# Spreading the per-block preparation of an S5 scan mixer over other pairs of groups

## Chip, cores and metric

The kernel runs on one core of a Trainium2 chip. The metric is the time of one execution in device microseconds (us). Shown is the median of three runs of the kernel before, and beside it one profiled execution with its own time and trace.

## The reference, cut to what matters

One inference step of a two-layer backbone runs over 1024 sample tokens and 128 prompt tokens with 1024 channels. Layer 0 mixes the tokens with a state-space scan (S5): the 1024 channels are 64 groups of 16, each with 64 complex states and two directions.

```
lam = lax.complex(lam_re, lam_im); dt = exp(log_dt)[:, None]
abar = exp(lam * dt)
bbar = ((abar - 1.0) / lam)[..., None] * bmat
bu = einsum('blgc,gpc->blgp', u, bbar)        # plus abar*h0 at the edge
h = associative_scan(h[t] = abar * h[t-1] + bu[t])     # per direction
y_d = real(einsum('gcp,blgp->blgc', cmat, h))
out = gated(gelu(y_0 + y_1 + ssm_d * u))
```

Behind it come a ConvFFN, a Fourier mixer (layer 1) and another ConvFFN. The change touches the S5 mixer alone, which is the first 305 us of some 2409.

## The kernel before

**Tiling.** `Ssm.run` works on 8 blocks `b` of 128 channels (8 groups each). A block has 4 pairs `pr` of two groups, so there are 32 steps, `i = 4*b + pr`. Time is cut into frames of 8 tokens: within a frame the recurrence is unrolled into matrices, and only the frame states are scanned. For each block the kernel needs

- `u` (`make_u`, `load_u`): the normed input of the block. TensorE transposes and scales token tiles of `xb` in three parts (L1487): part 0 is the prompt tile with one matmul, parts 1 and 2 are four sample tiles each. ScalarE writes them into one buffer `hb` (L1491, and L1495 and L1496 for two edge columns in part 0). Eight DMAs on the SP queue then read all of `hb` into `u` (L1502). There is only one `hb` and only one `xb`; `load_x` fills `xb` by DMA (L1341).
- `PT` (`make_p`): input matrices. Small factor products (L1418, L1423) and sums (L1429) are made on GpSimd, in block 1 on VectorE; TensorE transposes them, two transposes per half (L1437), and ScalarE copies them out (L1440). A half of `PT` serves two pairs.
- `CA` and `Bb` (`make_ca`): output matrices on GpSimd (L1359 to L1373), factors of the input on GpSimd (`bb[0]`) and VectorE (`bb[1]`, L1386 to L1396), edge copies on ScalarE (`ends`, L1377 to L1400).
- `T` (`make_t`): the kernel matrix inside a frame. TensorE makes it with 32 small matmuls (L1459, 64 rows by 32 columns, 128 wide; each shows as two instructions) into two banks, ScalarE copies it out (L1469 to L1471), GpSimd adds a diagonal (L1472, L1473), one DMA stores it to DRAM (L1475), and eight DMAs load it back skewed (L1478). These nine are on the SP queue too.
- `sn` and `cs` (`tables`): phases on VectorE (L1307, L1308, L983, L984), absolute value, sine and cosine on ScalarE (L1313, L1321).
- In block 0 alone, the powers and phases of all later blocks (`powers(rest, [second])`, shown under L951, with copies into `Q` and `G` on ScalarE, L1169 to L1173).

**Order.** The order on every engine is written out by hand: each engine and the SP queue take their instructions in program order, with waits that follow from the data and the buffers. Step `i` issues

1. `vmm(i+1)`: 16 matmul instructions of the next pair into one of two `V` buffers (L1515); it can start once step `i-1` has read that buffer (L1568);
2. a part of `make_u`, and in pair 0 `load_x`;
3. `scan(i)` on VectorE (L1556), `vin(i+1)` (L1537 to L1539 on VectorE, then four small ScalarE writes, L1541 to L1546, without which the next scan can't start), `vout(i)` (L1567, L1568), `decay(i+2)` on ScalarE (L1551);
4. `wmm(i-1)`: output matmuls with `T` (L1578) and `CA` (L1584), copied out by ScalarE (L1590);
5. the lists `fill` and `late`, in which the preparation of the next blocks is spread over the pairs.

In blocks 0 and 1 `vmm` also carries a slice of the adaLN projection (`ada_mm`, L1252, 32 instructions that walk over four column groups); its ScalarE copy `m_ada` (L1257) is one that L1537 of the same pair waits for.

The SP queue keeps eight DMA semaphores in turn, so a DMA is issued only when the one eight before it has landed. Before the change, block `b` does this:

```
pr 0: make_u(b+1) part 2, load_x(b+2), load_u(b+1), products half 0, tables s0, ends
pr 1: products half 1, transposes of half 0, wrap, abs, sine
pr 2: make_u(b+2) part 0, bb[0], CA 0..2, make_t(b+1) whole with its store and loads, cosine
pr 3: make_u(b+2) part 1, bb[1], CA 3..4, transposes of half 1
```

Of the kernel before, what the change touches and what calls it, by code (L numbers as in the profile page):

```python
# [12 lines left out]
AF = mybir.ActivationFunctionType  # L13
# [951 lines left out]
class Ssm:  # L965
# [478 lines left out]
    def make_t(self, b):  # L1444

        nc, sp, E = self.nc, self.sp, self.nc.gpsimd
        CA, Bb = self.CA[b], self.Bb[b]
        T = sp.tile([128, 8, 128], F32, tag="T", bufs=2, name="T")
        kc = self.sg.tile([128, 2, 240], F32, tag="kc", bufs=1, name="kc")
        k0 = self.sg.tile([128, 2, 16], F32, tag="k0", bufs=1, name="k0")  # L1450
        self.T[b] = T

        p = [self.bank("misc", 2) for _ in range(2)]
        for j in range(4):
            for a in range(2):
                rows = slice(64 * a, 64 * a + 64)
                for dr in range(2):
                    for ri in range(2):
                        nc.tensor.matmul(p[a][32 * j:32 * j + 32, dr * 128:dr * 128 + 128],  # L1459
                                         lhsT=Bb[rows, ri, 2 * j + dr].rearrange("p a b -> p (a b)"),  # L1460
                                         rhs=CA[rows, ri, 2 * j + dr, 2 * dr:2 * dr + 8].rearrange("p a b -> p (a b)"),
                                         start=ri == 0, stop=ri == 1)
        return lambda: self.store_t(b, p, T, kc, k0)

    def store_t(self, b, p, T, kc, k0):
        nc, sp, E = self.nc, self.sp, self.nc.gpsimd
        A = nc.scalar.activation
        for a in range(2):
            A(kc[:, a, 0:128], p[a][:, 128:256], AF.Copy)  # L1469
            A(k0[:, a], p[a][:, 0:16], AF.Copy)  # L1470
            A(kc[:, a, 128:240], p[a][:, 16:128], AF.Copy)  # L1471
        E.tensor_tensor(k0, k0, self.DD[:, b], OP.add)  # L1472
        E.tensor_tensor(kc[:, :, 112:128], kc[:, :, 112:128], k0, OP.add)  # L1473
        o = self.kd.offset + b * 2 * 128 * 240
        nc.sync.dma_start(bass.AP(tensor=self.kd.tensor, offset=o, ap=[[240, 128], [128 * 240, 2], [1, 240]]), kc)  # L1475
        for t in range(8):
            src = bass.AP(tensor=self.kd.tensor, offset=o + (7 - t) * 16, ap=[[240, 16], [32 * 240, 8], [1, 128]])
            nc.sync.dma_start(T[16 * t:16 * t + 16], src)  # L1478
# [125 lines left out]
    def run(self):  # L1604
# [3 lines left out]
        call = lambda fs: [f() for f in fs]  # L1608
        rest = slice(16, NG)
# [38 lines left out]
        ca1, ends1, bb = self.make_ca(1)  # L1648
        call(bb)
        self.diagonal()  # L1650
        self.make_t(0)()
        self.loads(2)
        n = 32
        for i in range(n + 1):
# [4 lines left out]
            if pr == 0 and n1 and b:  # L1659
                self.make_u(b + 1, parts=(2,))  # L1660
                if n2:
                    self.load_x(b + 2)
            elif pr > 1 and n2:
                self.make_u(b + 2, parts=(pr - 2,))
            if i < n:
                self.scan(i)
            if i + 1 < n:
# [14 lines left out]
                self.made.__exit__(None, None, None)  # L1682
            fill, late = [], []
            if pr == 0:
                if n1 and b:
                    self.load_u(b + 1)
                if b:
                    self.store_y(b - 1)
                if n1:
                    pp, tr = self.make_p(b + 1)  # L1690
                    fill = list(pp[0])
                    if b:
                        tb = self.tables(b + 1)
                        fill += tb[:1]
                if n1 and b:
                    late = [ends]
                if not b:
                    self.make_u(1)
                    self.load_u(1)
                    self.load_x(2)  # L1700
                    tb = self.tables(1)
                    fill += tb[:2] + ca1
                    second = Later(self.nc.vector)
                    self.phases(second, rest)
                    self.phases16(second, rest)
                    late = tr[0] + tb[2:3] + [lambda: self.powers(rest, [second]), ends1]
            if pr == 1:
                if n1:
                    fill = list(pp[1])
                    late = tr[0] + tb[1:3] if b else tb[3:]  # L1710
                if n2:
                    if b + 3 < 8:
                        self.loads(b + 3)
            if pr == 2:
                if n1:
                    late = [lambda: self.make_t(b + 1)()]
                    if b:
                        late += tb[3:]
                if n2:
                    ca, ends, bb = self.make_ca(b + 2)  # L1720
                    bb[0](self.nc.gpsimd if b else self.nc.vector)
                    fill = ca[:3]
            if i == 7:
                late = [self.last_frame]
            if pr == 3 and n1:
                late += tr[1]
                if n2:
                    bb[1]()
                    fill = ca[3:]
            if i >= 27:  # L1730
                late.append(lambda: self.n.early(i - 27))
            call(fill)
# [157 lines left out]
```

## Time and profile before

| | us |
|---|---|
| median of three runs (2411.02 to 2411.6) | 2411.51 |
| the profiled execution's own time | 2410.76 |
| its span, first to last instruction | 2408.9 |
| TensorE busy over the span | 2284.9 (95%) |
| VectorE busy over the span | 1469.9 (61%) |
| mixer loop, scan of step 0 to the last output matmul | 45.8 to 305 |

The profiled execution is 0.75 us below the median; 1.9 us of its time lie outside the span. Busy shares over the whole span belong mostly to the FFN stages; what a change in the mixer is worth has to be read from the mixer's own stretch. Rows of a timeline give start, duration, engine, line, operation, output and inputs, count, and in brackets the idle time just before and what ended it. PEclk is the granted TensorE clock as a share of 2.4 GHz.

### The profile page before, as it was taken

Reading aid. Unit: us, or ns where it says so; the run is one execution under the profiler, and the core shown is the slowest. Engines: PE = TensorE matmul, PEld = TensorE weight load, DVE = VectorE, ACT = ScalarE, POOL = GpSimd, SP = SyncE. Lnnn points to the kernel's source line nnn. Section 1 sums busy time; section 2 is a strip of 40 time slices with the busy share of each in tenths; the row PEclk is TensorE's granted clock in tenths of the full one; section 3 lists DMA queues with packets and bytes.
Section 4 is the critical chain, followed back from the end, with each engine's and each line's share of the span. In section 5 each row is a group of like instructions: output and inputs, shape, how many; then the busy total and the mean of one; then the engine's idle time right before and its main releaser. Section 6 shows DMA issues by size and latency. Waiting matters only on the chain.

```text
span 2408.9 us, 35526 instructions
## 1 busy us (share of the span) xinstructions
PE 2284.9 (95%) x14658; PEld 2207.7 (92%) x14658; DVE 1469.9 (61%) x2327; ACT 879.4 (37%) x1352; POOL 726.9 (30%) x486
## 2 busy tenths in 40 slices
PE   4788899999999999999999999999999999999996
PEld 4677797879999999999999999999999999999996
DVE  8888868895654556445553664764456455554556
ACT  5566653235232223322232354542223322232234
POOL 6588412363221122211221254521112211221124
PEclk9899999999999999999999999999999999999998
DMA  6443496661111111111110131121011101111112
GB/s 221 121 95 91 114 322 225 216 217 32 49 53 36 36 35 53 45 36 35 44 53 27 53 108 36 48 68 36 27 44 53 44 27 44 44 53 36 36 36 79
DMA packets 94520, 182.31 MB, mean 76 GB/s; under 512 B 16948, under 2 KB 57204, under 8 KB 93336
## 3 DMA queue, kind: packets, MB, share of 16 engines
q1 hardware_dynamic: 90824, 170.67, 22.9%
q0 software_dynamic: 2096, 6.62, 0.8%
q8 instruction: 116, 1.90, 0.3%
q10 hardware_dynamic: 1440, 2.75, 0.3%
q14 instruction: 44, 0.36, 0.0%
HBM read 163.70 MB, written 11.53 MB: 73 GB/s over the span
## 4 chain that ended last, share of the span: by engine, by line
PE 73%; DVE 17%; issue 4%; DMA 3%; ACT 2%; POOL 1%; SPq 1%; DVEq 0%; ACTq 0%; POOLq 0%
PE acc L199 64%; DVE c L308 3%; PE f L199 3%; PE f L839 2%; DVE dh L602 2%; DVE dl L602 2%; DMA w_ada<-w_ada 1%; PE misc L1459 1%; PE f L749 1%; DVE X L363 1%; DMA X<-xT 1%; PE y L1584 1%; DVE V L1538 1%; DVE X L364 1%; DVE V L1539 1%
## 5 line engine op out<-in xcount | busy, mean ns | idle before, releaser
L199 PE MATMUL acc<-h,uh 128*128 128x384 f32 (+1 forms) x4992 | 1014.0, 338 | 0.5 <-ACT ysb L1590 0.5
L199 PEld LDWEIGHTS acc<-h,uh 128*128 128x128 f32 x4992 | 884.2, 188 | 14.2 <-issue 10.9
L183 POOL TENSOR_TENSOR ul<-raw,uh 128x1024 fp32r<-128x1024 f32 x104 | 279.5, 2688 | 1232.1 <-ACT uh L182 1232.1
L199 PE MATMUL acc<-h,ul 128*128 128x384 f32 (+1 forms) x2496 | 571.3, 337 | 0.0
L308 DVE SCALAR_TENSOR_TENSOR c<-t,cw,c 128x896 f32<-128x896 f32 x704 | 347.2, 562 | 202.4 <-ACT c L305 202.4
L199 PEld LDWEIGHTS acc<-h,ul 128*128 128x128 f32 x2496 | 448.3, 189 | 0.0
L182 ACT ACTIVATE uh<-raw 128x1024 fp32r<-128x1024 f32 x108 | 113.7, 1053 | 549.6 <-PE acc L199 495.8
L300 DVE COPY wb<-acc 128x2 f32<-128x2 f32 x88 | 13.9, 158 | 405.8 <-PE acc L199 405.8
L363 DVE SCALAR_TENSOR_TENSOR X<-acc,MOD,X 128x768 f32<-128x768 f32 x168 | 169.8, 1010 | 118.3 <-PE acc L199 118.3
L199 PE MATMUL acc<-gh,dh 128*128 128x384 f32 x960 | 220.8, 337 | 18.4 <-DVE X L365 18.4
L199 PE MATMUL acc<-gl,dh 128*128 128x384 f32 x960 | 218.6, 335 | 0.0
L199 PE MATMUL acc<-gh,dl 128*128 128x384 f32 x960 | 218.3, 335 | 0.0
L199 PEld LDWEIGHTS acc<-gh,dh 128*128 128x128 f32 x960 | 168.8, 188 | 26.9 <-PE acc L199 23.6
L336 ACT ACTIVATE gh<-c 128x1152 fp32r<-128x1152 f32 x44 | 51.4, 1169 | 329.2 <-DVE c L331 290.9
L199 PEld LDWEIGHTS acc<-gh,dl 128*128 128x128 f32 x960 | 171.4, 188 | 0.0
L199 PEld LDWEIGHTS acc<-gl,dh 128*128 128x128 f32 x960 | 171.2, 188 | 0.0
L303 ACT ACTIVATE t<-t,wb 128x1024 f32<-128x1024 f32 x88 | 101.4, 1153 | 152.5 <-DVE t L301 152.5
L183 POOL TENSOR_TENSOR dl<-raw,dh 128x1024 fp32r<-128x1024 f32 x40 | 99.8, 2515 | 165.0 <-ACT dh L182 165.0
L305 ACT ACTIVATE c<-t,cb,cw 128x1152 f32<-128x1152 f32 x88 | 118.9, 1351 | 2.9
L301 DVE TENSOR_TENSOR t<-acc,R 128x1152 f32<-128x1152 f32 x88 | 118.6, 1348 | 0.0
L326 ACT ACTIVATE c<-c 128x1152 f32<-128x1152 f32 x44 | 51.4, 1167 | 152.3 <-DVE c L308 152.3
L602 DVE SCALAR_TENSOR_TENSOR dl<-w_ada,SC,dl 128x1024 f32<-128x1024 f32 x50 | 88.9, 1816 | 0.0
(316 smaller groups left out, 2601.6 us busy)
## 6 DMA issues: line engine op xcount, KB each, us to landing
raw<-w_up SPq DMA_DIRECT2D x88, 512.0 KB, 3.6
w_ada<-w_ada SPq DMA_DIRECT2D x80, 512.0 KB, 4.9
raw<-w_down SPq DMA_DIRECT2D x44, 512.0 KB, 3.6
w_ada<-w_ada SPq DMA_DIRECT2D x8, 1024.0 KB, 5.9
raw<-w_glu SPq DMA_DIRECT2D x16, 512.0 KB, 4.6
u<-hb SPq DMA_DIRECT2D x64, 73.0 KB, 3.7
y_scratch<-ysb SPq DMA_DIRECT2D x8, 584.0 KB, 3.7
xt<-x SPq DMA_DIRECT2D x9, 512.0 KB, 8.1
```

What stands on the lines that cost most here:

```text
L182: nc.scalar.activation(hi, raw, AF.Copy)
L183: (E or nc.gpsimd).tensor_tensor(lo, raw, hi.bitcast(F32), OP.subtract)
L199: mm(outs[j], lhsT=w, rhs=r[j], start=first and i == 0, stop=last and i == 2)
L301: nc.vector.tensor_tensor(t.rearrange("p (a b) -> p a b", a=3), p[:, :, :384], self.R.rearrange("p (a b) -> p a b", a=3), OP.mult)
L303: nc.scalar.activation(t[:, :NS], t[:, :NS], AF.Identity, bias=wb[:, 0:1])
L305: nc.scalar.activation(c, t, AF.Identity, bias=cb[:, ui:ui + 1], scale=w(1))
L308: nc.vector.scalar_tensor_tensor(o, a, w(i), o, op0=OP.mult, op1=OP.add)
L326: nc.scalar.activation(c, c, AF.Silu)
L336: nc.scalar.activation(gh, c, AF.Copy)
L363: nc.vector.scalar_tensor_tensor(v, p[:, 0:2, :384], s(0), v, op0=OP.mult, op1=OP.add)
L602: nc.vector.scalar_tensor_tensor(o, i, a, o, op0=OP.mult, op1=OP.add)
L839: nc.tensor.matmul(o, lhsT=l, rhs=x, start=kd not in seen, stop=n == last[kd], skip_group_check=True)
```

## The change

`make_t` is cut into two steps, `part(0)` and `part(1)`, one per half of the states' rows, each into one bank with its own three ScalarE copies; within a part the four column groups `j` are the innermost loop. The store and the eight loads of `T` follow `part(1)`. In block `b` the work is now placed so:

```
pr 0: make_u(b+1) part 2, load_x(b+2), load_u(b+1), products half 0, tables s0, transposes of half 1 of block b, ends
pr 1: make_u(b+2) part 0, bb[0], products half 1, transposes of half 0, wrap, abs, sine
pr 2: bb[1], CA 0..2, part(0) of T(b+1), cosine
pr 3: make_u(b+2) part 1, CA 3..4, part(1) of T(b+1), store and loads of T(b+1)
```

In block 0 the tables of block 1 move from pair 0 to pair 1, the powers of the later blocks from pair 0 to pair 2, and `make_ca(2)` from pairs 2 and 3 to pair 3.

```diff
@@ make_t @@
-        p = [self.bank("misc", 2) for _ in range(2)]
-        for j in range(4):
-            for a in range(2):
+        A = nc.scalar.activation
+
+        def part(a):
+
+            def f():
+                p = self.bank("misc", 2)
                 rows = slice(64 * a, 64 * a + 64)
                 for dr in range(2):
                     for ri in range(2):
-                        nc.tensor.matmul(p[a][32 * j:32 * j + 32, dr * 128:dr * 128 + 128],
...
-        return lambda: self.store_t(b, p, T, kc, k0)
...
+                        for j in range(4):
+                            nc.tensor.matmul(p[32 * j:32 * j + 32, dr * 128:dr * 128 + 128],
...
+                A(kc[:, a, 0:128], p[:, 128:256], AF.Copy)
+                A(k0[:, a], p[:, 0:16], AF.Copy)
+                A(kc[:, a, 128:240], p[:, 16:128], AF.Copy)
+            return f
+        return [part(0), part(1), lambda: self.store_t(b, T, kc, k0)]
@@ run @@
-            elif pr > 1 and n2:
-                self.make_u(b + 2, parts=(pr - 2,))
+            elif pr in (1, 3) and n2:
+                self.make_u(b + 2, parts=(pr // 2,))
...
             if pr == 0:
-                if n1 and b:
-                    self.load_u(b + 1)
                 if b:
+                    late = list(tr[1])
+                    if n1:
+                        self.load_u(b + 1)
+                        late.append(ends)
                     self.store_y(b - 1)
+                else:
+                    self.make_u(1)
+                    self.load_u(1)
+                    self.load_x(2)
                 if n1:
                     pp, tr = self.make_p(b + 1)
                     fill = list(pp[0])
+                    tb = self.tables(b + 1)
                     if b:
-                        tb = self.tables(b + 1)
                         fill += tb[:1]
-                if n1 and b:
-                    late = [ends]
+                    else:
+                        fill += ca1
+                        late = list(tr[0])
+            if pr == 1 and n1:
+                if n2 and b:
+                    ca, ends, bb = self.make_ca(b + 2)
+                    bb[0](self.nc.gpsimd)
+                fill = pp[1] + tb[:0 if b else 1]
+                late = (tr[0] if b else [ends1]) + tb[1:3]
+                if b + 3 < 8:
+                    self.loads(b + 3)
+            if pr == 2 and n1:
+                mt = self.make_t(b + 1)
+                late = mt[:1] + tb[3:]
                 if not b:
-                    self.make_u(1)
...
                     second = Later(self.nc.vector)
                     self.phases(second, rest)
                     self.phases16(second, rest)
-                    late = tr[0] + tb[2:3] + [lambda: self.powers(rest, [second]), ends1]
...
+                    self.powers(rest, [second])
+                elif n2:
+                    bb[1]()
                     fill = ca[:3]
+            if pr == 3 and n1:
+                if b and n2:
+                    fill = ca[3:]
+                elif not b:
+                    ca, ends, bb = self.make_ca(2)
+                    bb[0](self.nc.vector)
+                    bb[1]()
+                    fill = ca
+                late = mt[1:]
             if i == 7:
-                late = [self.last_frame]
-            if pr == 3 and n1:
-                late += tr[1]
-                if n2:
-                    bb[1]()
-                    fill = ca[3:]
+                late.append(self.last_frame)
```

## Rows read from the trace of the kernel before

**Rows 1.** Groups of instructions, 45 to 304 us; columns: busy us, mean ns | idle before, releasers

```profile
L1556 DVE TENSOR_TENSOR_SCAN V<-dec,V 128x592 f32<-128x592 f32 x32 | 44.3, 1386 | 1.9 <-ACT V L1546 1.5 <-ACT a L1272 0.4
...
L1538 DVE TENSOR_TENSOR V<-V,cs 128x584 f32<-128x584 f32 x31 | 24.0, 775 | 2.9 <-ACT cs L1321 2.0
...
L1537 DVE TENSOR_TENSOR B<-V,sn 128x584 f32<-128x584 f32 x31 | 23.4, 753 | 26.3 <-PE V L1515 18.0 <-ACT m_ada L1257 8.2
```

**Rows 2.** Timeline of VectorE: one block, and the scans of steps 6 and 22

```profile
119.36 1.38 DVE L1556 TENSOR_TENSOR_SCAN V<-dec,V 128x592 f32<-128x592 f32 x1
...
180.41 1.38 DVE L1556 TENSOR_TENSOR_SCAN V<-dec,V 128x592 f32<-128x592 f32 x1
...
185.71 1.40 DVE L1556 TENSOR_TENSOR_SCAN V<-dec,V 128x592 f32<-128x592 f32 x1 [0.31 <-ACT V L1546]
190.08 0.77 DVE L1537 TENSOR_TENSOR B<-V,sn 128x584 f32<-128x584 f32 x1 [2.98 <-PE V L1515]
...
194.02 0.40 DVE L1386 TENSOR_TENSOR Bb<-Bm,beta 128x128 f32<-128x128 f32 x1
...
196.40 1.39 DVE L1556 TENSOR_TENSOR_SCAN V<-dec,V 128x592 f32<-128x592 f32 x1
...
241.13 1.38 DVE L1556 TENSOR_TENSOR_SCAN V<-dec,V 128x592 f32<-128x592 f32 x1
```

**Rows 3.** Busy time of the engines in two blocks' time, with granted clock

```profile
180.00:240.00 60.00, 51.68 (x606) 46.05 (x606) 51.80 (x67) 37.16 (x121) 52.53 (x48) 0.95 0.37 91
```

**Rows 4.** Timeline of TensorE, block 0 (first row) and one later block

```profile
93.96 1.08 PE L1252 MATMUL V<-w_ada,SC 128*32 128x128 f32 x32
...
178.74 1.43 PE L1515 MATMUL V<-u,PT 128*64 128x146 f32 x16 [2.46 <-DVE C L1568]
...
181.79 2.84 PE L1584 MATMUL y<-C,CA 64*128 64x146 f32 x32
184.56 4.32 PE L1459 MATMUL misc<-CA,Bb 64*32 64x128 f32 x64
188.82 1.22 PE L1515 MATMUL V<-u,PT 128*64 128x146 f32 x16
...
191.55 2.26 PE L1584 MATMUL y<-C,CA 64*128 64x146 f32 x32
```

**Rows 5.** Timeline of the SP queue around two stores of the kernel matrix

```profile
189.96 0.37 SPq L1475 DMA_DIRECT2D k_scratch<-kc  x1
193.30 3.68 SPq L1478 DMA_DIRECT2D T<-k_scratch  x8
197.10 0.39 SPq L1341 DMA_DIRECT2D xb<-x  x1
...
227.52 0.39 SPq L1341 DMA_DIRECT2D xb<-x  x1
228.06 6.29 SPq L1502 DMA_DIRECT2D u<-hb  x8
```

**Rows 6.** Waits of the SP queue, 60 to 300 us (total, times, longest)

```profile
SPq L1478 <- DMA k_scratch<-kc: 13.7, 7, 2.9
```

**Rows 7.** The eight loads of `u`, 227 to 236 us: issue to landing

```profile
DMA to landing us min/median/max: 2.6/3.7/5.5
```

**Rows 8.** Waits put ahead of the writes of `hb` (line L1491), whole span

```profile
L1491 ACTq EVENT_SEMAPHORE  x28: 38/38/38, 50.1 to 241.5; - x28
```

**Rows 9.** Timeline of ScalarE in pairs 1 and 2 of one block

```profile
177.44 0.17 ACT L1541 ACTIVATE Fin<-V 128x4 f32<-128x4 f32 x1 [4.75 <-DVE V L1539]
...
184.22 0.44 ACT L1491 ACTIVATE hb<-misc,b,a 128x128 f32<-128x128 f32 x1
...
185.61 0.96 ACT L1551 ACTIVATE dec<-mask,r 128x296 f32<-128x296 f32 x2
186.48 0.39 ACT L1590 ACTIVATE ysb<-y 128x292 f32<-128x292 f32 x1
...
189.30 1.84 ACT L1321 ACTIVATE cs<-wa,hpi 128x516 f32<-128x516 f32 x4
```

More of the change, by code (lines that the diff above doesn't have):

```diff
@@ L1458, in make_t, with store_t @@
                     for ri in range(2):
-                        nc.tensor.matmul(p[a][32 * j:32 * j + 32, dr * 128:dr * 128 + 128],
-                                         lhsT=Bb[rows, ri, 2 * j + dr].rearrange("p a b -> p (a b)"),
-                                         rhs=CA[rows, ri, 2 * j + dr, 2 * dr:2 * dr + 8].rearrange("p a b -> p (a b)"),
-                                         start=ri == 0, stop=ri == 1)
-        return lambda: self.store_t(b, p, T, kc, k0)
-    def store_t(self, b, p, T, kc, k0):
-        nc, sp, E = self.nc, self.sp, self.nc.gpsimd
[L1467 to L1471, printed above, removed]
+                        for j in range(4):
+                            nc.tensor.matmul(p[32 * j:32 * j + 32, dr * 128:dr * 128 + 128],
+                                             lhsT=Bb[rows, ri, 2 * j + dr].rearrange("p a b -> p (a b)"),
+                                             rhs=CA[rows, ri, 2 * j + dr, 2 * dr:2 * dr + 8].rearrange("p a b -> p (a b)"),
+                                             start=ri == 0, stop=ri == 1)
+                A(kc[:, a, 0:128], p[:, 128:256], AF.Copy)
[3 more added lines that the diff above has]
+        return [part(0), part(1), lambda: self.store_t(b, T, kc, k0)]
+    def store_t(self, b, T, kc, k0):
+        nc, sp, E = self.nc, self.sp, self.nc.gpsimd
         E.tensor_tensor(k0, k0, self.DD[:, b], OP.add)
@@ L1650, in run @@
         self.diagonal()
-        self.make_t(0)()
+        call(self.make_t(0))
         self.loads(2)
@@ L1691, in run @@
                     fill = list(pp[0])
+                    tb = self.tables(b + 1)
                     if b:
-                        tb = self.tables(b + 1)
                         fill += tb[:1]
-                if n1 and b:
-                    late = [ends]
-                if not b:
-                    self.make_u(1)
[L1699 to L1702, printed above, removed]
+                    else:
[12 more added lines that the diff above has]
+                late = mt[:1] + tb[3:]
+                if not b:
                     second = Later(self.nc.vector)
@@ L1705, in run @@
                     self.phases16(second, rest)
-                    late = tr[0] + tb[2:3] + [lambda: self.powers(rest, [second]), ends1]
[L1707 to L1710, printed above, removed]
-                if n2:
[L1712 to L1721, printed above, removed]
-                    fill = ca[:3]
-            if i == 7:
-                late = [self.last_frame]
-            if pr == 3 and n1:
-                late += tr[1]
-                if n2:
-                    bb[1]()
-                    fill = ca[3:]
+                    self.powers(rest, [second])
+                elif n2:
+                    bb[1]()
+                    fill = ca[:3]
+            if pr == 3 and n1:
[7 more added lines that the diff above has]
+                late = mt[1:]
+            if i == 7:
+                late.append(self.last_frame)
             if i >= 27:
```

## The prediction

> **What bounds the kernel now.** I looked first at where VectorE waits in the mixer loop, because every pair of groups passes through it. Grouped over the loop, it waits 30.1 us: the first product of a pair (L1537) 26.3 us, of which 18.0 for `vmm` on TensorE and 8.2 for the projection's copy, the next product 2.0 for the cosine table, the scan 1.9 for ScalarE [rows 1]. That is the ceiling of any gain here: the change takes no work from VectorE. The timeline of one block shows where it sits. From step 6 to step 22 a block takes (241.13 - 119.36) / 4 = 30.44 us, and its waits come at one place, between pairs 2 and 3: 0.31, then 2.98 [rows 2], then a sixth of the 2.0 for the cosine: 3.6 us. So VectorE's own work is about 26.8 us per block; a pair with nothing extra takes 185.71 - 0.31 - 180.41 = 5.0 [rows 2].
>
> The 2.98 us are `make_t`: its 64 instructions hold TensorE from 184.56 for 4.32 us, and the `vmm` that the next pair needs starts at 188.82 behind them [rows 4]. TensorE, VectorE and GpSimd are each busy about 52 of 60 us in this stretch [rows 3], so none has much room.
>
> **The change, part by part.**
>
> *Split of `make_t`: gain.* A part has 32 instructions, with the four column groups innermost. The nearest row is the projection, 32 instructions of the same width over four column groups: 1.08 us [rows 4]. I take 1.05 for each part, 2.1 in place of 4.3; the upper bound is half the old time, 2.15 each. At either value `vmm` of pair 3 is in time, since `bb[1]`, from 194.02 to the scan at 196.40, 2.4 us [rows 2], now lies in pair 2 and gives TensorE that much more. So all 3.6 us per block go, if nothing takes their place. Transposes and products only change pair; TensorE and GpSimd have as much to do as before or less.
>
> *Store and loads of `T` one pair later: what is queued behind.* The store follows `part(1)` at the end of pair 3, where it stood in pair 2. On the SP queue the eight `T` loads wait for it to land, and `load_x` and the eight loads of `u`, issued in pair 0, stand behind them. From the store's issue:
> - to the first `T` load: seven waits of 13.7 us in all, 2.0 each [rows 6], and 0.4 of issue: 2.4; the block shown has 3.3 [rows 5].
> - eight `T` issues: 3.7; then `load_x` [rows 5].
> - from `load_x` at 227.52: the last of eight `u` loads is issued about 0.6 before 228.06 + 6.29, at 233.75, and the smallest landing, 2.6, is taken as its own: 236.35, 8.8 us after `load_x` [rows 5, 7]. With the largest landing, 5.5, it is 11.7.
>
> Sum: 2.4 + 3.7 + 8.8 = 14.9 us from store to last `u`; 18 at the upper ends.
>
> *Part 0 of `make_u` from pair 2 to pair 1: the new wait.* It writes `hb`, which the loads of the previous block's `u` may still be reading. The four waits ahead of each of seven such writes, 28 in all, are in the queue already [rows 8]; they cost nothing now because in pair 2 the loads have long landed. In pair 1 they haven't. By VectorE's pace the write would come some 7 us after the store, and it may come up to 11 us after it before VectorE waits; the loads land at 14.9. Behind it on ScalarE stand the four small writes that the scan of pair 2 needs: from 184.22 to the decay at 185.61, 1.4 us [rows 9]. So that scan starts 16.4 us after the store. TensorE waits too, for `xb`, some 12 us after the store.
>
> *From that scan to the next store.* ScalarE goes on through decay, output copy, two `PT` copies, absolute value and sine: from 177.44 to 184.22 it took 6.8, of which 0.8 lie before the scan. Then pair 2's small writes, decay and copy, 184.9 to 186.9, three copies of the kernel matrix (0.4) and the cosine (1.8): 10.0 us after the scan [rows 9]. VectorE reaches the product that needs the cosine after a pair (5.0), `bb[1]` (2.4), a scan (1.3) and a product (0.8): 9.5. So 0.5 more is lost. Then 1.5 for the rest of that product, 2.0 for small writes, decay and copy, 0.4 for copies and 0.6 for GpSimd's adds (cosine start 189.30 to store 189.96 [rows 5, 9]): the next store is issued 14.5 us after the scan. With waits between engines I take 14.9. One block: 16.4 + 14.9 = 31.3 us, where it took 30.44. The wait for `make_t` is replaced by a longer one.
>
> *TensorE's clock.* After an idle 2.46 us in pair 1 the output matmuls take 2.84 us where they take 2.26 ten us later [rows 4]; the granted clock averages 0.95 of 2.4 GHz [rows 3]. With the change TensorE stands some 5 us for `xb`. What lies behind is about what lies between 188.82 and 193.8, 5 us [rows 4], and must end 17.7 us after the store; at 2.4 GHz it ends at 17. Lower bound 0; upper bound all of it at 1.2 GHz, 5 us more, of which slack and cosine hide 1.2: 3.8 per block. The row is nearest to the low end, so 0.6 per block. The Trainium skill, "TensorE: Matmul & The Clock Gate", section "HAM oscillation — how this bites in real kernels", says that a matmul loop with a DMA wait in each round restarts each round at half clock. By that rule the cost would lie near the upper bound.
>
> *Block 0.* The powers (VectorE) move from pair 0 to pair 2; nothing is saved. The waits there are 8.2 and 0.4 now [rows 1]. After, by the same kind of walk: the `vmm` of step 2 queues behind transposes that end after VectorE's products, about 4; the projection's copy of step 3 stands behind the sine, 3; that of step 4 behind powers and cosine, 2; later ones 1.5. That is 10.5, less about 2.5 because the tables no longer run beside GpSimd's products: 8.0, an estimate that may be off by 3 either way.
>
> *Blocks 6 and 7.* Block 6 has no `load_x`, so its wait goes. In block 7, with pairs of 5.0 us, the late second-half transposes and the late `T` are met unhidden: about 2.8. The next stage's first loads are pushed back some 5 us on the SP queue, which I take as covered by its work till then.
>
> **Sum.** Waits before: 30.1. After: block 0 8.0; blocks 1 to 5, 5 x (31.3 - 26.8 + 0.6) = 25.5; block 7 2.8: 36.3. Difference +6.2 us, and all that follows the mixer starts later by it. On the profiled execution's 2410.8 this gives 2417.0; that execution is 0.75 below the median, so I forecast 2417.5.
>
> **The rivals.**
> - *The loads land in time: not slower.* Each us off the 14.9 is worth 5, one per block. At 13.7 the change is neutral; at 11 the waits of blocks 1 to 5 vanish, 10.8 us of waits remain, and the time is 2411.5 - 19.3 = 2392. For it: 2.4 and 8.8 each held a us of jitter, and ScalarE may have less ahead of it. Against it: 3.7 and 8.8 were met back to back. Chance 0.24, mostly near 2405.
> - *TensorE's clock takes the place.* With all work behind the wait at 1.2 GHz each block loses 3.8 in place of 0.6: 2417.5 + 16 = 2433. For it: the idle time doubles. Against it: slow stretches are short now. Chance 0.12. It is the case that the clock rule of the Trainium skill, cited above, describes.
> - *Nothing measurable.* A chain a little shorter, and block 0 better by its 3: 2410 to 2416. Chance 0.18.
>
> My forecast has the other 0.46; its own case spans 2413 to 2424. What a measurement of this kernel can tell from no change is about 0.2%, 4.8 us: under 2406.7 is faster, over 2416.3 slower. Faster: 0.19 of the first rival. Same: its other 0.05, the third's 0.18 and 0.08 at the forecast's lower edge, 0.31. Slower: the forecast's other 0.38 and the clock's 0.12, 0.50. The range, 2400 to 2431, leaves out the far ends of the first two rivals.
>
> **What would show it.** Right: in blocks 1 to 5 ScalarE's write of part 0 comes after the last `u` load lands; the scan of pair 2 waits for ScalarE 3 us or more; L1537 no longer waits 3 us in pair 3; each part is near 1.05 us; from store to store 31 to 32 us. Wrong: scans of pair 2 without that wait, blocks of about 27 us, or a step 6 more than 4 us away from 119.36 [rows 2].

## The result and the profile after

The changed kernel took 2432.89 us (median of 4 runs, 2431.52 to 2435.37), the kernel before 2411.27 beside it: ratio 1.0090, 95% interval 1.0077 to 1.0103, so 21.6 us slower. I had forecast 2417.5. The direction is right, the size is not, and the range (up to 2431) misses it. In the profiled executions the last scan of the mixer starts at 320.86 us instead of 298.57, 22.3 us later; the two executions are 24.6 us apart (2435.37 and 2410.76), so all but 2.3 us of the loss is in the mixer.

Where VectorE waits in the loop of the changed kernel, grouped by line as in [rows 1] (45 to 326 us; busy us, mean ns | idle before, releasers; the lines are two higher after the change):

```profile
L1558 DVE TENSOR_TENSOR_SCAN V<-dec,V 128x592 f32<-128x592 f32 x32 | 44.4, 1387 | 6.9 <-ACT V L1548 5.8 <-ACT a L1272 1.1
...
L1540 DVE TENSOR_TENSOR V<-V,cs 128x584 f32<-128x584 f32 x31 | 24.0, 774 | 2.6 <-ACT cs L1321 1.2
...
L1539 DVE TENSOR_TENSOR B<-V,sn 128x584 f32<-128x584 f32 x31 | 23.6, 761 | 33.3 <-PE V L1517 22.2 <-ACT m_ada L1257 11.1
```

The named waits are 22.2 + 11.1 + 5.8 + 1.2 + 1.1 = 41.4 us, 11 more than the 30.1 of before. That is half of the loss only. The other half is in the busy time. From the scan of step 6 to that of step 22, four blocks, the busy time of each engine in the kernel before (us, then PE, PEld, DVE, ACT, POOL, granted clock, DMA share, GB/s):

```profile
119.36:241.13 121.77, 104.28 (x1215) 91.80 (x1214) 104.44 (x134) 76.70 (x248) 103.31 (x97) 0.94 0.39 92
```

and between the same two scans in the changed kernel:

```profile
121.27:257.08 135.81, 108.28 (x1210) 93.76 (x1212) 114.65 (x132) 74.91 (x246) 106.27 (x99) 0.83 0.34 82
```

A block went from 30.44 to 33.95 us. VectorE has the same instructions, yet is busy 28.66 us per block where it was 26.11 (the 26.8 of the prediction is this with 0.7 of short gaps). Its idle time rose from 4.33 to 5.29. So 2.55 of the 3.51 us that a block lost are instructions of VectorE that became longer, and 0.96 are waits. The granted clock of TensorE fell as well, from 0.94 to 0.83.

One block of VectorE, from the scan of pair 1 on (start, us; idle before in brackets):

```profile
183.88 0.85 DVE L983 TENSOR_SCALAR wa<-w 128x896 f32<-128x896 f32 x1
184.76 2.04 DVE L984 TENSOR_TENSOR w<-w,wa 128x896 f32<-128x896 f32 x1
187.64 1.40 DVE L1558 TENSOR_TENSOR_SCAN V<-dec,V 128x592 f32<-128x592 f32 x1 [0.84 <-ACT V L1548]
191.77 0.77 DVE L1539 TENSOR_TENSOR B<-V,sn 128x584 f32<-128x584 f32 x1 [2.74 <-PE V L1517]
...
195.41 2.38 DVE L1386 TENSOR_TENSOR Bb<-Bm,beta 128x128 f32<-128x128 f32 x1
197.71 0.28 DVE L1387 TENSOR_TENSOR Bx<-Bm,beta 128x128 f32<-128x128 f32 x1
```

L1386, the first product of `bb[1]`, took 0.40 us in [rows 2] and takes 2.38 here. Over the four blocks L1386, L1387 and L1388 together take 13.7 us where they took 6.8; the four table lines (L1307, L1308, L983, L984) take 21.6 where they took 18.7. GpSimd around that moment:

```profile
170.57 0.25 POOL L1474 TENSOR_TENSOR k<-k,DD 128x32 f32<-128x32 f32 x1 [6.74 <-ACT k L1467]
...
193.27 1.93 POOL L1372 TENSOR_TENSOR CA<-Qt,Cx 128x1024 f32<-128x1024 f32 x1
195.28 2.36 POOL L1373 TENSOR_TENSOR CA<-CA,CAt 128x1024 f32<-128x1024 f32 x1
204.91 0.25 POOL L1474 TENSOR_TENSOR k<-k,DD 128x32 f32<-128x32 f32 x1 [7.27 <-ACT k L1467]
```

Its last product of `CA` runs from 195.28 to 197.64; L1386 ends 0.15 us behind it, and L1387 then takes 0.28. From the adds at 170.57 to the end of that product GpSimd has no gap above 0.15 us; then it stands 7.27 us until ScalarE has copied the next part of the kernel matrix. The new wait that I had predicted is there too. The SP queue, and ScalarE's write of part 0 (pair 1):

```profile
171.18 0.37 SPq L1477 DMA_DIRECT2D k_scratch<-kc  x1
173.54 3.65 SPq L1480 DMA_DIRECT2D T<-k_scratch  x8
177.29 0.39 SPq L1341 DMA_DIRECT2D xb<-x  x1
177.78 6.31 SPq L1504 DMA_DIRECT2D u<-hb  x8
...
205.51 0.37 SPq L1477 DMA_DIRECT2D k_scratch<-kc  x1
```

```profile
186.14 0.46 ACT L1493 ACTIVATE hb<-misc,b,a 128x128 f32<-128x128 f32 x1 [6.08 <-DMA u<-hb]
```

From the store to that write 14.96 us (predicted 14.9), to the scan of pair 2 16.46 (16.4), from there to the next store 17.87 (14.9). TensorE meanwhile waits 3.46 us for `xb` and then works at 1.2 GHz (granted clock 0.50 of 2.4 GHz from 184 to 186 us):

```profile
183.65 0.77 PE L1489 MATMUL misc<-rstd,xb 128*128 128x128 f32 x2 [3.46 <-DMA xb<-x]
...
185.32 4.24 PE L1586 MATMUL y<-C,CA 64*128 64x146 f32 x32
...
194.54 1.08 PE L1462 MATMUL misc<-CA,Bb 64*32 64x128 f32 x32
```

The output matmuls take 4.24 us where they take 2.26 at 2.4 GHz, and VectorE waits 2.74 us for the `vmm` behind them. A part of the kernel matrix takes 1.08 us (predicted 1.05). So two causes stand in the stretch that came out 3 us too long, the clock and GpSimd, and one profile does not separate them. The second rival gave 2433 us for the clock alone, which is the measured time.

### The profile page after: what moved, and what is told of

Same layout as the page of the kernel before. It is cut to its first block, busy times and chain, and to the rows that moved or that the text cites. A ratio compares the mean times of both kernels' runs of the same rounds, so it can differ in the third digit from the quotient of the medians.

```text
span 2433.6 us, 35540 instructions
## 1 busy us (share of the span) xinstructions
PE 2291.9 (94%) x14658; PEld 2207.7 (91%) x14658; DVE 1480.2 (61%) x2327; ACT 878.5 (36%) x1352; POOL 726.4 (30%) x486
## 4 chain that ended last, share of the span: by engine, by line
PE 73%; DVE 15%; DMA 4%; issue 4%; ACT 2%; SPq 1%; POOL 1%; DVEq 0%; ACTq 0%; POOLq 0%
PE acc L199 63%; DVE c L308 3%; PE f L199 2%; PE f L839 2%; DVE dh L602 1%; DVE dl L602 1%; PE y L1586 1%; DMA w_ada<-w_ada 1%; DMA xb<-x 1%; PE V L1517 1%; PE f L749 1%; DVE X L363 1%; DVE X L364 1%; DMA X<-xT 1%; DVE V L1540 1%
## 5 line engine op out<-in xcount | busy, mean ns | idle before, releaser
L199 PEld LDWEIGHTS acc<-h,uh 128*128 128x128 f32 x4992 | 884.7, 188 | 16.2 <-issue 12.5
```

Of the source, the lines that this page charges most:

```text
L199: mm(outs[j], lhsT=w, rhs=r[j], start=first and i == 0, stop=last and i == 2)
```

## Experiments

All in one table first; times in us. Per block is from the scan of step 6 to that of step 22, divided by four, with VectorE's busy and idle part; the ratio is to the kernel before on the same chip.

| kernel | per block | busy | idle | last scan | ratio (95%) |
|---|---|---|---|---|---|
| before | 30.44 | 26.11 | 4.33 | 298.57 | 1 |
| changed | 33.95 | 28.66 | 5.29 | 320.86 | 1.0090 (1.0077 to 1.0103) |
| e1: part 0 in pair 2 | 32.48 | 30.50 | 1.98 | 315.34 | 1.0071 (1.0050 to 1.0092) |
| e2: TensorE kept busy, first try | 33.83 | 27.82 | 6.02 | 320.37 | 1.0099 (1.0078 to 1.0120) |
| e4: part 0 put aside | 33.23 | 28.18 | 5.06 | 321.60 | 1.0088 (1.0068 to 1.0109) |
| e5: TensorE kept busy | 33.79 | 29.25 | 4.54 | 317.05 | 1.0084 (1.0067 to 1.0101) |
| e6: `bb[1]` in pair 3 | 31.39 | 26.85 | 4.54 | 309.01 | 1.0052 (1.0037 to 1.0067) |
| e9: e5 and e6 | 32.10 | 26.82 | 5.28 | 308.42 | 1.0057 (1.0041 to 1.0074) |
| e7: e1 and e6 | 29.26 | 26.86 | 2.40 | 297.12 | 1.0003 (0.9993 to 1.0013) |
| p1: e1, `CA` products as fills | 26.57 | 25.57 | 0.99 | 287.23 | 0.9968 (0.9955 to 0.9981) |
| e3: before, split alone | 28.42 | 26.06 | 2.36 | 282.36 | 0.9935 (0.9917 to 0.9953) |
| e8: e3, cosine first | 29.56 | 27.97 | 1.59 | 288.51 | 0.9977 (0.9967 to 0.9987) |
| f2: e3, cosine between | 29.87 | 27.89 | 1.99 | 290.68 | 0.9989 (0.9978 to 1.0000) |
| g1: e8, all `CA` products in pair 2 | 31.48 | 28.05 | 3.43 | 298.57 | 0.9999 (0.9983 to 1.0015) |

**e1: the wait taken away.** Only the pair of part 0 goes back:

```diff
-            elif pr in (1, 3) and n2:
-                self.make_u(b + 2, parts=(pr // 2,))
+            elif pr > 1 and n2:
+                self.make_u(b + 2, parts=(pr - 2,))
```

> The changed kernel with one line undone: part 0 of make_u is made in pair 2 again, not in pair 1. Theory (the wait of part 0 for xb and for the loads of u, with TensorE at 1.2 GHz behind it, makes the block longer): ScalarE's wait before its first write of hb and TensorE's wait for xb in pair 1 are gone, a block falls from 33.95 us to 28.5 to 29.5 (VectorE's own 26.8 and about 2 for vmm at half clock in pairs 0 and 1, where TensorE still idles between pairs 3 and 0), five blocks give back 22 to 27 us: 2406 to 2411 us. Rival (the block is longer because of the other moves: transposes and products a pair later, store at the end of pair 3): a block stays above 32 us and the time above 2423.

The theory missed. VectorE's idle time fell to 1.98 us per block as it said, but the block fell by 1.47 us only, for VectorE's busy time rose to 30.50. The rival's numbers hold (a block above 32 us, 2433 us), though the move that does it, `bb[1]`, is none of those that it names. VectorE and, behind it, GpSimd in one block of this kernel:

```profile
187.36 1.82 DVE L1386 TENSOR_TENSOR Bb<-Bm,beta 128x128 f32<-128x128 f32 x1
189.10 2.01 DVE L1387 TENSOR_TENSOR Bx<-Bm,beta 128x128 f32<-128x128 f32 x1
191.15 2.40 DVE L1388 TENSOR_TENSOR Bb<-Bb,Bx 128x128 f32<-128x128 f32 x1
```

```profile
186.67 2.36 POOL L1371 TENSOR_TENSOR CA<-CAt,CA 128x1024 f32<-128x1024 f32 x1
188.99 1.98 POOL L1372 TENSOR_TENSOR CA<-Qt,Cx 128x1024 f32<-128x1024 f32 x1
191.04 2.36 POOL L1373 TENSOR_TENSOR CA<-CA,CAt 128x1024 f32<-128x1024 f32 x1
200.13 0.25 POOL L1474 TENSOR_TENSOR k<-k,DD 128x32 f32<-128x32 f32 x1 [6.73 <-ACT k L1467]
```

GpSimd's products end at 189.03, 190.97 and 193.40, VectorE's at 189.18, 191.11 and 193.55: each 0.14 or 0.15 us behind the one of GpSimd that it met. The wait for the loads had kept VectorE out of GpSimd's way; without it VectorE arrives early and stands there.

The mean hides how little was won. From the scan of step 12 on a block of e1 takes 33.85 us, three times in a row, though no wait for loads is left in it; in the changed kernel the same three blocks take 34.34, 33.95 and 34.36. The rest of the gain lies in the steps before. What sets the 33.85 us is a second chain that closes once per block. GpSimd works 27.12 us without a stop from its adds to the kernel matrix (166.28) to the end of its last product of `CA` (193.40). `bb[1]` ends just behind that product; then come the scan of pair 3, VectorE's products, ScalarE's small writes and its copies of `part(1)`, and only then GpSimd's next adds, 6.73 us after its last product. I call this the GpSimd chain; the other is the load chain, from the store through the loads of `u` to the next store.

**e2 and e5: TensorE kept at work.** `keep(n)` issues n matmuls of the identity with itself that nobody reads. In e2 pair 3 has 8 of them, in the `y` bank; in e5 7, in a bank of their own (`True`):

```diff
             elif pr in (1, 3) and n2:
+                if pr == 1 and b:
+                    self.keep(11)
                 self.make_u(b + 2, parts=(pr // 2,))
...
-                late = mt[1:]
+                late = mt[1:2] + [lambda: self.keep(7, True)] + mt[2:]
```

> The changed kernel with work for TensorE where it idles in blocks 1 to 7: 11 matmuls of the identity with itself (about 0.29 us each) in pair 1 ahead of part 0 of make_u, and 8 behind the second part of make_t in pair 3, into columns of the y bank that nobody reads. The waits for xb and for the loads of u stay as they are. Theory (the clock is what my sum had too small: 2.65 us of a block's 33.95): the granted clock stays at 2.4 GHz through pairs 0 to 2, vmm takes 1.22 us everywhere, a block falls to 31.3 us, which is the chain of waits that I worked out, and five blocks give back 13 us: about 2420 us. Rival (the chain through the queue, ScalarE and GpSimd is itself 34 us long and the clock is hidden in it): the clock is at 2.4 GHz as well, but a block stays within 0.7 us of 33.95 and the time is 2430 to 2436.

The block fits the rival (33.83 us), the time lies a little above its range (2438.5 us). The output matmuls behind the wait for `xb` take 2.26 us in all four blocks. But the run was flawed: in pair 3 the added matmuls waited for ScalarE's copy out of the `y` bank, the next `vmm` stood behind them, and VectorE waited 4.3 to 4.5 us for it in each of the four blocks. Hence e5, in which the matmuls of pair 3 wait for no such copy:

> The changed kernel with TensorE kept at work where it idles in blocks 1 to 7, this time so that nothing has to wait for the added matmuls: 11 of the identity with itself in pair 1 ahead of part 0 of make_u, 7 behind the second part of make_t in pair 3 into a bank of their own. Theory now (port: VectorE's products with both inputs in SBUF stand until the product that GpSimd has begun is over, and bb[1] in pair 2 lies beside the 1.9 to 2.4 us products of CA): the clock stays at 2.4 GHz and the 2.7 us that VectorE waits for vmm in pair 2 go, but bb[1] comes the earlier into GpSimd's products and takes 5 us in place of 3.3: a block of 32 to 33.5 us, the last scan of the mixer 2 to 8 us earlier than the changed kernel's 320.9, 2425 to 2432 us. Rival (clock: the missing 2.65 us per block are TensorE's): a block of 31.3 us, the last scan 13 us earlier, 2420 us or below.

The granted clock between the two scans is back at 0.94, that of before, and a block takes 33.79 us. The rival fails (31.3 us, 2420 us or below); the theory's block and time are missed by a little (33.5 and 2432 us at most, 33.79 and 2433.0 measured). But the clock was not kept up everywhere. Behind the wait for `xb` the output matmuls ran at full speed in the third of the four blocks alone; in the others they took 3.78 to 3.93 us. TensorE in pair 1 of the second and of the third block:

```profile
184.73 3.93 PE L1586 MATMUL y<-C,CA 64*128 64x146 f32 x32
...
218.21 2.26 PE L1586 MATMUL y<-C,CA 64*128 64x146 f32 x32
```

So the third block is the test of the clock, one block and no more. From the scan of step 16 to that of step 20, in the changed kernel and in e5 (columns as above):

```profile
203.82:237.77 33.95, 28.23 (x306) 24.42 (x306) 28.44 (x34) 18.91 (x63) 26.74 (x24) 0.80 0.34 84
```

```profile
203.82:237.80 33.98, 27.57 (x342) 23.74 (x342) 30.48 (x35) 18.64 (x63) 26.77 (x24) 1.00 0.36 84
```

The clock is at 2.4 GHz throughout, VectorE's 4.6 us of waits for `vmm` are gone, and the block takes as long as before. L1386 to L1388 take 5.68 us in place of 3.00 and end behind GpSimd's last product as they did, and the scan of pair 2 waits 3.0 us for ScalarE in place of 0.4: the GpSimd chain is as long as it was (its adds come at 204.91 and 238.89 us, in the changed kernel at 204.91 and 238.86), and the clock is not what that block lost. VectorE and ScalarE in pair 1 to 2 of the second block show the load chain beside it:

```profile
188.36 1.40 DVE L1558 TENSOR_TENSOR_SCAN V<-dec,V 128x592 f32<-128x592 f32 x1 [2.40 <-ACT V L1548]
190.88 0.77 DVE L1539 TENSOR_TENSOR B<-V,sn 128x584 f32<-128x584 f32 x1 [1.12 <-PE V L1517]
...
195.98 2.34 DVE L1388 TENSOR_TENSOR Bb<-Bb,Bx 128x128 f32<-128x128 f32 x1
```

```profile
186.85 0.46 ACT L1493 ACTIVATE hb<-misc,b,a 128x128 f32<-128x128 f32 x1 [7.74 <-DMA u<-hb]
```

The wait for `vmm` is 1.12 us in place of 2.74, but the scan of pair 2 waits 2.40 us for ScalarE, which waits for the loads of `u`; and `bb[1]` meets more of GpSimd's products. The last scan is 3.8 us earlier, and 3.0 of that lie in block 7, which has no such wait: steps 28 to 31 take 17.51 us where the changed kernel takes 20.49. There the output matmuls behind the late `T` take 0.74 and 2.26 us in place of 1.31 and 4.06: 2.4 us are the clock's.

**e4: part 0 put aside.** The write of part 0 goes to a small tile, copied into `hb` in pair 2:

```diff
-                self.make_u(b + 2, parts=(pr // 2,))
+                self.make_u(b + 2, parts=(pr // 2,), aside=pr == 1)
+            if pr == 2 and n2:
+                self.put_u()
```

> The changed kernel, where part 0 of make_u in pair 1 is put down in a small tile of its own and copied into hb in pair 2, so that ScalarE does not wait for the loads of u in pair 1; TensorE still waits for xb there. Theory (both waits end close together, the one for u last): in pair 1 ScalarE writes when TensorE has done, about 1.7 us earlier than it does now, the scan of pair 2 comes as much earlier, the clock behind TensorE's wait stays at 1.2 GHz: 1 to 1.7 us per block, 2424 to 2428 us. Rival 1 (the wait for u is all there is to it, as I had written): 3 us or more per block, 2418 or below. Rival 2 (what sets the block is TensorE behind xb, the write of hb lies beside it): no change, 2431 to 2434.

The second rival holds: a block is 0.7 us shorter, the time the same. ScalarE no longer waits for `u`, but TensorE still waits 16.2 us for `xb` in the four blocks (14.9 in the changed kernel), and the wait comes back at `vmm`, 17.0 us where it was 13.5. The two waits stand side by side; taking one away leaves the other. The GpSimd chain is untouched: GpSimd stops 6.74 to 7.60 us per block, in the changed kernel 6.74 to 7.27.

**e6: `bb[1]` back in pair 3**, where GpSimd stands idle until the kernel matrix is copied:

```diff
                 elif n2:
-                    bb[1]()
                     fill = ca[:3]
...
                 if b and n2:
+                    bb[1]()
                     fill = ca[3:]
```

> The changed kernel with bb[1] of VectorE put back from pair 2 to pair 3, where GpSimd stands idle from the end of the products of CA to the next kernel matrix. All else as in the changed kernel, waits for the loads of u and for xb included. Theory (port): the five instructions of bb[1] take 0.3 to 0.5 us each, 1.8 us in place of 3.8 per block, the stretch from the scan of pair 2 to the next store loses 3 us, and since bb[1] now lies in the wait for the loads, a block falls by 2 to 3 us: last scan at 306 to 311 us, 2418 to 2424 us. Rival (their length is their own, or what they lose lies beside TensorE's late vmm): a block stays within 1 us of 33.95, 2428 us or more.

As the theory said: 2.56 us per block, last scan at 309.0. Of the 2.56 us 1.81 are busy time of VectorE and 0.75 waits. `bb[1]`, all five instructions, falls from 16.0 to 6.1 us in the four blocks, less the 3.1 us by which the table lines rise, to 24.7: they are what meets GpSimd now. `bb[1]` in one block:

```profile
197.21 0.28 DVE L1386 TENSOR_TENSOR Bb<-Bm,beta 128x128 f32<-128x128 f32 x1
197.41 0.28 DVE L1387 TENSOR_TENSOR Bx<-Bm,beta 128x128 f32<-128x128 f32 x1
197.73 0.29 DVE L1388 TENSOR_TENSOR Bb<-Bb,Bx 128x128 f32<-128x128 f32 x1
```

In this kernel the load chain comes out at the length that I had worked out, though not in every part: `bb[1]` lies in pair 3, and VectorE waits 1.25 us for the cosine in the block shown, where I had 0.5. The stores of the kernel matrix and ScalarE's write between them:

```profile
167.29 0.37 SPq L1477 DMA_DIRECT2D k_scratch<-kc  x1
...
198.91 0.37 SPq L1477 DMA_DIRECT2D k_scratch<-kc  x1
```

```profile
182.41 0.46 ACT L1493 ACTIVATE hb<-misc,b,a 128x128 f32<-128x128 f32 x1 [7.86 <-DMA u<-hb]
```

15.1 us to the write, 16.6 to the scan of pair 2 (183.92), 15.0 from there to the next store: 31.62 from store to store, 31.39 per block on the mean, where I had 31.3. TensorE's clock averages 0.87 in it.

**e9: both**, the added matmuls of e5 and `bb[1]` moved:

> The changed kernel with bb[1] in pair 3 and TensorE kept at work in its idle stretches (the two single runs together); the wait for the loads of u stays. Theory (the clock cost nothing in the changed kernel because waits for the loads and GpSimd's port lay over it; with bb[1] out of the way it shows): VectorE's waits for vmm, 12.9 us with bb[1] alone moved, fall under 6, the last scan comes 3 to 7 us before the 309.0 of that run, 2414 to 2420 us. Rival (it stays hidden behind the loads of u): last scan within 2 us of 309.

The rival holds. VectorE's waits for `vmm` fell from 12.9 to 8.4 us, those for ScalarE's small writes rose from 6.9 to 9.8, and a block is no shorter (32.10). But here too the output matmuls behind the wait for `xb` ran at full speed in the third block alone (2.26 us; 3.88 to 4.27 in the others). From step 16 to step 20 that block takes 30.74 us and 31.12 in e6, so in the one block that shows it the clock is worth 0.4 us behind the wait for loads.

**e7: e1 and e6 together**, both diffs as above:

> The changed kernel with both undone: part 0 of make_u in pair 2 and bb[1] in pair 3. With part 0 alone undone VectorE's waits fell to 2 us per block, but its own work rose to 30.5 us beside GpSimd. Theory (port and wait are the two terms, and nothing else of size): bb[1] takes under 2.5 us, VectorE's own work is 26.8 to 28 us per block, its waits 2 to 3: a block of 29 to 30.5, last scan at 299 to 306 us, 2410 to 2418 us. Rival (another term in the moved transposes and products): a block above 31.5 us, last scan later than 310.

The theory holds, at its low edge: 29.26 us per block and the time of before (1.0003); the last scan, 297.1, is 2 us ahead of its range. Alone the two moves gave 5.5 and 11.9 us at the last scan; together they give 23.7, more than the sum. The two chains stand side by side, and the longer one sets the block: e1 takes away the load chain and leaves the 33.85 us of GpSimd's, e6 takes away the GpSimd chain and leaves the 31.4 us of the loads, e7 takes away both. So undoing these two moves takes back the whole net loss. What e7 keeps of the change (the split, the transposes, GpSimd's products, the late store, the powers) is worth nothing on balance. Since the split alone is worth 16 us (e3, below), the other moves that e7 keeps take that back: against e3, 8.1 us by step 6, 3.3 in the next four blocks and 4.4 from step 28 to 31, less 1.1 between. Which of them does so was not taken apart further.

**p1: is it GpSimd, and what of it?** Kernel e1, with fills in the place of GpSimd's products of `CA`:

```diff
+        if b > 1:
+            st = [lambda o=o: E.memset(o, 0.25) for o in (re, re, re, im, im)]
```

> The changed kernel with part 0 of make_u in pair 2 (as in the first run), and GpSimd's five products of CA of every block from the third on left out: fills of a constant into the same places stand in for them, so GpSimd writes but reads nothing there. Theory (port: it is GpSimd's reading that VectorE's two-input products wait for): bb[1] in pair 2 takes 0.28 to 0.45 us for each of its five instructions, also where a fill runs beside it, VectorE's own work falls from 30.5 to 27 to 28.5 us per block, a block to 28.5 to 30 us, last scan at 299 to 306 us where it was 315.3 with part 0 alone moved back. Rival (any work of GpSimd slows VectorE, or the products are long of themselves): the first three of bb[1] stay above 1 us where a fill runs, last scan later than 310.

The theory holds, and by more than I gave it. GpSimd and VectorE in one block:

```profile
175.03 4.87 POOL L1376 MEMSET CA<- 128x1024 f32 x5
```

```profile
177.55 0.28 DVE L1389 TENSOR_TENSOR Bb<-Bm,beta 128x128 f32<-128x128 f32 x1
177.75 0.28 DVE L1390 TENSOR_TENSOR Bx<-Bm,beta 128x128 f32<-128x128 f32 x1
178.07 0.29 DVE L1391 TENSOR_TENSOR Bb<-Bb,Bx 128x128 f32<-128x128 f32 x1
```

The five fills run from 175.03 to 179.90, and the same three instructions that took 1.82, 2.01 and 2.40 us in e1 take 0.28, 0.28 and 0.29 beside them. VectorE's busy time falls from 30.50 to 25.57 us per block. GpSimd also has less to do (a fill takes 1.0 us), so the time is no price; the durations are what counts.

**e3: the split alone**, put into the kernel before:

```diff
-                    late = [lambda: self.make_t(b + 1)()]
+                    late = self.make_t(b + 1)
```

with `make_t` as in the change.

> The kernel before with one part of the change: make_t in two parts with the four column groups innermost, both still one after the other in pair 2, everything else where it was. Theory (the split alone frees the vmm of pair 3 by 2.2 us per block): each part takes about 1.08 us, VectorE's wait of 3 us in pair 3 falls to about 0.9, and what is left is partly the cosine: 2 us per block in seven blocks, 2396 to 2400 us. If the cosine on ScalarE is late next: 2404 to 2408. Rival (the duration does not depend on the order of the column groups, the moved parts are short for another reason): the two parts take 2.15 us each and the time stays at 2411.

The last scan is 16.2 us earlier, the ratio 0.9935: faster than both kernels, with a time (2398.9 us) in the theory's range. Each part takes 1.08 us here as well, both in the same pair, so 2.2 us replace the 4.3 of [rows 4]: the short duration comes with the new loops and not with the new place. The wait for `vmm` in the loop is gone; the cosine is late in its place (VectorE's waits, 45 to 322 us: total, times, longest):

```profile
DVE V L1540 <- ACT cs L1321: 9.7, 6, 1.6
```

**e8, f2 and g1: the cosine earlier.** Three tries to take these 9.7 us as well: the cosine ahead of both parts, between them, and ahead of both with all of GpSimd's products of `CA` issued in pair 2. The edit of e8, against e3 (f2 has `late[1:1] = tb[3:]` in its place, g1 is e8 with `fill = ca` in pair 2 and no `fill` in pair 3):

```diff
-                    late = self.make_t(b + 1)
-                    if b:
-                        late += tb[3:]
+                    late = self.make_t(b + 1)
+                    if b:
+                        late = tb[3:] + late
```

> The kernel before with the split alone, both parts in pair 2, and the cosine put ahead of the two parts on ScalarE. With the split alone VectorE's wait for vmm in pair 3 was gone and the wait for the cosine had come in its place: 9.7 us in six blocks. Theory (the cosine is what is late next, by 1.6 us per block, and the copies of the kernel matrix behind it have room): the wait for the cosine falls under 3 us in all, the last scan comes 5 to 8 us earlier than with the split alone (282.4), 2391 to 2394 us. Rival (the kernel matrix is then late: GpSimd waits 1.8 us longer for its copies, and the products behind it meet VectorE's): no gain over the split alone, 2396 to 2402 us.

The wait for the cosine fell to 4.3 us, but the rival decided, and beyond its range (2405.7 us): the last scan came 6.2 us later than in e3. GpSimd waits 2.28 us for the late copies, its last product of `CA` then meets `bb[1]`, and L1388 takes 2.33 us.

> The kernel before with the split alone, both parts in pair 2, and the cosine between the two parts on ScalarE. With the cosine ahead of both, the kernel matrix was 1.84 us later, GpSimd waited for it, its last product of CA then met bb[1], and 6 us were lost. Theory (a copy group of 0.6 us ahead is less than the slack of either side): the wait for the cosine falls from 9.7 to about 5 us in all, the kernel matrix is about 0.9 us later, bb[1] loses under 0.6 us per block: last scan within 2 us of 282.4, 2396 to 2401 us. Rival (the meeting of GpSimd's product with bb[1] decides as soon as the kernel matrix is later at all): last scan at 285 to 289 us, 2402 to 2406 us.

Again the rival, worse than its range (290.7, 2412.1 us): GpSimd waits 2.29 us for the copies here too, and L1387 takes 2.46 us beside its last product.

> The kernel with the split and the cosine ahead of both parts (last scan 288.5, 2405.7 us), and GpSimd's five products of CA all issued in pair 2, ahead of its adds to the kernel matrix, where two of them stood behind those adds in pair 3. Theory (what was lost there is the last two products of CA running beside bb[1], because GpSimd stood 2.3 us for the late copies of the kernel matrix): without that stop the products are over at about the time bb[1] begins, L1388 and L1396 fall from 2.33 and 1.15 us to under 1.2 and 0.4, the cosine's wait stays under 1 us per block: a block of 27 to 28 us where it took 29.56, last scan at 273 to 281 us, 2387 to 2396 us. Rival (the products come early enough to meet the tables or the adds come too late for the store): a block of 28.4 us or more, last scan later than 282.4, no better than the split alone.

The theory misses, and the rival holds. `bb[1]` is indeed undisturbed (L1388 0.29 us), but the products of `CA`, now without a stop in between, meet the tables of pair 1, and each holds up the other:

```profile
177.17 1.15 DVE L983 TENSOR_SCALAR wa<-w 128x896 f32<-128x896 f32 x1
178.36 2.69 DVE L984 TENSOR_TENSOR w<-w,wa 128x896 f32<-128x896 f32 x1
```

```profile
180.19 3.10 POOL L1371 TENSOR_TENSOR CA<-CAt,CA 128x1024 f32<-128x1024 f32 x1
```

In one block of e8 L983 and L984 took 0.62 and 1.23 us, and GpSimd's product 2.38. The best version found is e3; each of the three moves around it lost a part or all of what it had won, each time with a meeting of VectorE and GpSimd in the trace (in g1 VectorE also waits 11.7 us for `vmm`, and never in e3).

## Why the prediction missed

- *The split.* Right: 1.08 us per part (1.05 predicted), and the wait for `make_t` is gone. e3 shows that alone it wins 16 us.
- *Store, loads of `T`, `xb` and `u`.* Right in length: 14.96 us from store to the write of part 0 (14.9), 16.46 to the scan (16.4), in e6 15.0 from there to the next store (14.9) and 31.4 us per block (31.3). But it was not the longest chain. The scan of pair 2 waits 0.37 to 2.46 us for ScalarE, where I had named 3 or more as a sign of being right, and with that wait taken away (e1) a block from step 12 on still takes 33.85 us.
- *VectorE's own work, "about 26.8 us per block".* This step failed. I carried it over from before as if an instruction brought its duration along, and priced `bb[1]` in its new place with the 2.4 us of its old one [rows 2]. In pair 2 it lies beside GpSimd's products of `CA` and ends behind the last of them, however early it begins. Busy time per block rose by 2.55 us, 10.2 in four blocks; the five instructions of `bb[1]` rose by 6.8, the tables by 2.8. The same instructions keep VectorE busy for 25.57 us per block in p1 and 30.50 in e1, so the waits were no ceiling either, as I had taken them to be.
- *From the scan of pair 2 to the next store, 14.9 us.* It took 17.87, by the same step: my walk followed ScalarE and VectorE, and GpSimd, whose products hold `bb[1]`, was not in it. "TensorE and GpSimd have as much to do as before or less" counted GpSimd's work and not when it runs. e6, which takes `bb[1]` out of that stretch, has 15.0 there and a block 2.56 us shorter.
- *TensorE's clock, 0.6 us per block.* The clock did fall (0.83), as in the rival, and its 2433 us were the measured time. But in the one block of e5 in which TensorE stayed at 2.4 GHz throughout, the block took 33.98 us for 33.95: the GpSimd chain covered the clock. That it cost nothing in the other blocks is argued from the same chain: e2, where the output matmuls ran at full speed behind the wait in all four (33.83 us per block), had a wait of its own. In block 7 it cost 2.4 us, where the sum had none for it. A right number is no proof of its mechanism. The Trainium skill, "TensorE: Matmul & The Clock Gate", section "HAM oscillation — how this bites in real kernels", describes a loop with a load wait in each round that restarts each round at half clock. The trace agrees with that (4.24 us for 2.26 behind the wait for `xb`); that it would set the time here, it does not.
- *Block 0.* Right within its margin of 3 us, and in its terms: 12.2 us of waits where I had 10.5, and 1.6 us less busy time where I had 2.5. Step 6 comes 1.9 us later than in [rows 2], where the sum had it 0.6 earlier.
- *Blocks 6 and 7.* From step 22 to 28 1.1 us were lost and from 28 to 31 5.3, where I had 2.8 for block 7: the late transposes and the late `T` are there, with the clock's 2.4 us on top.

Together 1.9 + 14.0 + 1.1 + 5.3 = 22.3 us; the 14.0 are four blocks of 3.51, of which the sum had 1.46.

**Carry over.** When an instruction of VectorE with both inputs in SBUF is moved, look at what GpSimd runs at the new place: it lasts there until the GpSimd product that it meets has ended, and the profile shows that as busy time, not as a wait. A wait that is taken away lets work arrive earlier, and what it then meets is part of the price; so try causes alone and together. A rival whose number comes out right still needs the run that takes away its cause alone.

## What the runs showed of the hardware

VectorE's products with both inputs in SBUF stand still while a product of GpSimd runs that began before them: L1387 takes 0.28 us where GpSimd idles (e6) and 2.46 us where it runs a product of 2.51 (f2), and ends 0.15 us behind that. The other way about too: a product of GpSimd took 3.10 us for 2.38 where it met L984. VectorE's products that take one input from PSUM do not feel it: L1539 takes 0.77 us in the lines of the changed kernel and of e5, with GpSimd's products of `CA` running. Two inputs in SBUF are not needed, though: L1307, a copy of one tile, takes 0.23 us in a block of e5, where GpSimd's product ended 0.07 us behind its start, and 1.35 us in a block of e6, where it began 0.02 us behind the start of a GpSimd sum of 1.28 us and ended 0.08 behind the end of it.

The Trainium skill, "SBUF — State Buffer", section "Who interferes with whom", states this as a rule: an instruction of VectorE with two SBUF inputs contends with one of GpSimd that reads SBUF, "not with one that only writes it"; the lock on the shared ports is exclusive, and issue order decides who blocks. The traces agree on each point: 2.40 us beside a product (e1) and 0.29 beside a fill (p1), L1387 held by the product that began before it (f2), a product held by L984 that began before it (g1).
